# Three of four k-groups by seven products, two of the block sums added by accumulating loads

## The chip, the cores and the metric

The kernel runs on one core of one Trainium2 chip. The time is device microseconds (us) of one execution of the whole program; the median of three executions of the kernel before is 2425.75 us (2423.84 to 2429.18). The engines of the core are TensorE (PE, with its weight loads as PEld), VectorE (DVE), ScalarE (ACT), GpSimd (POOL) and SyncE (SP, which here only issues DMAs).

## The reference

Two transformer blocks follow each other on x of 256 tokens by 2048, all in float32. The two feed-forward networks (FFN) are what matters here; each has a hidden width of 5632 = 11 chunks of 512:

```python
def conv_ffn(x, w_gate, w_up, conv_w, conv_b, w_down):       # first block
    hg = x @ w_gate
    hg = causal_depthwise_conv(hg, conv_w, width=3) + conv_b
    return (jax.nn.gelu(hg, approximate=True) * (x @ w_up)) @ w_down

x = x + (jax.nn.silu(h @ w_gate[l]) * (h @ w_up[l])) @ w_down[l]   # second block
```

Before them stand the projections, the mixers and the output projections of each block, behind the first FFN a gated projection, and at the end a norm.

## The kernel before

**Precision.** A float32 product is made of three matmuls of a type with a shorter mantissa. Each 512 KB weight block (128 partitions by 1024) is loaded raw, ACT writes its rounded half `whi` (L133 or L603), and DVE the rest `wlo = raw - whi` (L134 or L604). PE then runs whi, wlo and whi again against the high and low halves of the activations. `whi` and `wlo` have five buffers each, so the split of a block waits until PE has used the block five before it. The raw blocks lie in three buffers `raw` and four buffers `t4k`; `load_weight` (L102) issues their loads on SP's queue in order.

**Tiling.** One block covers KG = 2 tiles of 128 of the contraction and 512 columns. The 256 tokens are two halves of 128. A plain product of a block is 2 (k tiles) x 2 (token halves) x 3 = 12 matmuls of 512 columns.

**Seven products for eight.** `pair_product` (L607) makes the gate and the up chunk `u` together. The 2048 of the contraction are 16 tiles, or four k-groups: group gp takes the blocks gp and gp + 4 of both weights, b11, b12 (gate and up of gp) and b21, b22 (gate and up of gp + 4). Eight block products of a half of the tokens (8 x 6 = 48 matmuls) can be made as seven (42 matmuls) out of sums of blocks, in the way of Strassen and Winograd: t1 = b11 + b12, t2 = t1 + b22, t3 = b12 + b22, t4 = t2 + b21. The products and their banks are p1 (b11), p2 (b21), q3 (b22), q5 (t1), q7 (t3), q6 (t2) and q4 (t4); the eight-bank PSUM is full while they run. DVE makes the four sums (L648, L652, L659, L662). The groups in MIXED = (0, 2) go this way, groups 1 and 3 plainly. The activations' own sums (`strassen_operands`, L570) are made once in each FFN. Chunks 0 and 1 are made plainly (`product`).

**Order of the work.** `ffn` (L731) goes over groups of chunks, (0, 1), (2, 3) ... (8, 9), (10): a chunk is made, and behind it stands half of the down products of the chunk group before (`drain`). The hidden activations of a chunk (16 transposes and the gating, `fill`) run as side work: each `pump()` in `product` emits a step of it. `pair_product` has no pump. A scheduler orders each engine's instructions; `tc.high_priority()` moves splits and sums ahead.

**After the groups** p1, q6, q5 and q7 are combined and p2, q3, q4 and x22 added (L672 to L679).

Of the kernel before, what the change touches and what calls it, by code (L numbers as in the profile page):

```python
# [14 lines left out]
ALU = mybir.AluOpType  # L15
# [8 lines left out]
KG = 2  # L24
# [29 lines left out]
def two_blocks_kernel(ctx: ExitStack, tc: tile.TileContext, A: dict, out: bass.AP):  # L54
# [12 lines left out]
    def t2k():  # L67
        return new([P, 512], "t2k", 8)
# [7 lines left out]
    def chunk_tile(dt=F32):  # L76
        return new([P, 2, 512], "pj", 8, dt)

    def psum(tag="tp"):
        return ps.tile([P, 512], F32, tag=tag, bufs=4, name=f"{tag}_{next(uid)}")  # L80
# [21 lines left out]
    def load_weight(w, c, g):  # L102
        deep = ahead[0] and next(loads) % 7 > 2
        raw = new([P, KG * 512], "t4k", 4) if deep else new([P, KG * 512], "raw", 3)
        nc.sync.dma_start(raw[:, : KG * w.widths[c]], w.block(c, g))
        return raw
# [35 lines left out]
    def add_side(gen, after=0):  # L142
        side.append([tick[0] + after, gen])
# [452 lines left out]
        add_side(make(), 1)  # L596
        return sx

    MIXED = (0, 2)

    def split_raw(raw):
        hi, lo = new([P, KG * 512], "whi", 5, F32R), new([P, KG * 512], "wlo", 5, F32R)
        act(hi, raw, AF.Copy)  # L603
        dve.tensor_tensor(lo, raw, hi.bitcast(F32), op=ALU.subtract)  # L604
        return hi, lo

    def pair_product(wa, wb, u, xs, sx):  # L607

        p1, q5, p2, q3 = (psum("acc") for _ in range(4))
        q6, q7, x22, q4 = (psum() for _ in range(4))
        ca, cb = chunk_tile(), chunk_tile()
        add, sub = ALU.add, ALU.subtract
        begun = set()

        def products(bank, st, wt, stop):
            (shi, slo), (hi, lo) = st, wt
            for j in range(KG):
                wh, wl = hi[:, j * 512 : (j + 1) * 512], lo[:, j * 512 : (j + 1) * 512]  # L620
                pe.matmul(bank, shi(j), wh, start=id(bank) not in begun, stop=False)  # L621
                begun.add(id(bank))
                pe.matmul(bank, shi(j), wl, start=False, stop=False)  # L623
                pe.matmul(bank, slo(j), wh, start=False, stop=stop and j == KG - 1)  # L624

        def plain(g, m):
            tok = slice(m * P, (m + 1) * P)
            return lambda j: xs[g * KG + j][0][:, tok], lambda j: xs[g * KG + j][1][:, tok]

        def mixed(gp, i):  # L630
            fs = slice(i * P, (i + 1) * P)
            return lambda j: sx[gp * KG + j][:, 0, fs], lambda j: sx[gp * KG + j][:, 1, fs]

        half = KT // KG // 2
        for gp in range(half):
            if gp not in MIXED:
                for w_, banks in ((wa, (p2, q4)), (wb, (q3, x22))):
                    for g in (gp, gp + half):
                        wt = split_weight(w_, u, g)
                        for m in range(2):  # L640
                            products(banks[m], plain(g, m), wt, g == KT // KG - 1)
                continue
            last = gp == MIXED[-1]
            b11, b12, b21, b22 = (load_weight(w_, u, g) for g in (gp, gp + half) for w_ in (wa, wb))
            with tc.high_priority():
                f11 = split_raw(b11)
                t1 = b11
                dve.tensor_tensor(t1, b11, b12, op=ALU.add)  # L648
                f21 = split_raw(b21)
                f22 = split_raw(b22)  # L650
                t3 = b12
                dve.tensor_tensor(t3, b12, b22, op=ALU.add)  # L652
            products(p1, plain(gp, 0), f11, last)
            products(p2, plain(gp + half, 0), f21, gp == half - 1)
            products(q3, mixed(gp, 3), f22, gp == half - 1)
            with tc.high_priority():
                ft1 = split_raw(t1)
                t2 = b22
                dve.tensor_tensor(t2, t1, b22, op=ALU.add)  # L659
                ft3 = split_raw(t3)  # L660
                t4 = b21
                dve.tensor_tensor(t4, t2, b21, op=ALU.add)  # L662
            products(q5, mixed(gp, 0), ft1, last)
            products(q7, mixed(gp, 2), ft3, last)
            with tc.high_priority():
                ft2 = split_raw(t2)
            products(q6, mixed(gp, 1), ft2, last)
            with tc.high_priority():
                ft4 = split_raw(t4)
            products(q4, plain(gp + half, 1), ft4, gp == half - 1)  # L670
            if last:
                act(ca[:, 0], p1, AF.Copy)  # L672
                dve.tensor_tensor(ca[:, 1], ca[:, 0], q6, op=add)
                dve.scalar_tensor_tensor(cb[:, 0], ca[:, 1], -1.0, q5, ALU.mult, add)
                dve.tensor_tensor(ca[:, 1], ca[:, 1], q7, op=add)
                dve.tensor_tensor(cb[:, 1], cb[:, 0], q7, op=sub)

        for t, bank in ((ca[:, 0], p2), (cb[:, 0], q3), (ca[:, 1], q4), (cb[:, 1], x22)):
            dve.tensor_tensor(t, t, bank, op=add)  # L679
        return ca, cb  # L680

    def conv_unit(u, xs, r, sx):
        if sx is None:
            gt = evacuate(product(W["gate"], u, xs), r)
            ut = evacuate(product(W["up"], u, xs), r)
        else:
            gt, ut = pair_product(W["gate"], W["up"], u, xs, sx)
            for t in (gt, ut):
                for m in range(2):
                    act(t[:, m], t[:, m], AF.Copy, scale=r[:, m : m + 1])  # L690

        def hidden(kk):
            i = u * 4 + kk
            t = psum()
            fs = slice(kk * P, (kk + 1) * P)
            tg = transpose_pair([gt[:, m, fs] for m in range(2)], t)
            tu = transpose_pair([ut[:, m, fs] for m in range(2)], t[:, T:])
            cv = t1k()
            act(cv, tg, AF.Identity, scale=CONV[2][:, i : i + 1], bias=CONVB[:, i : i + 1])
            dve.scalar_tensor_tensor(cv[:, 1:], tg[:, : T - 1], CONV[1][:, i : i + 1], cv[:, 1:], ALU.mult, ALU.add)  # L700
            dve.scalar_tensor_tensor(cv[:, 2:], tg[:, : T - 2], CONV[0][:, i : i + 1], cv[:, 2:], ALU.mult, ALU.add)
            act(cv, cv, AF.Gelu_apprx_tanh)
            dve.tensor_tensor(cv, cv, tu, op=ALU.mult)
            return stationary(cv, "hid")

        return hidden

    def swiglu_unit(u, xs, r, sx):
        if sx is None:
            sg = evacuate(product(W["gate2"], u, xs), r, func=AF.Silu)  # L710
            up = product(W["up2"], u, xs)
        else:
            sg, ut = pair_product(W["gate2"], W["up2"], u, xs, sx)
            for m in range(2):
                act(sg[:, m], sg[:, m], AF.Silu, scale=r[:, m : m + 1])
            up = [ut[:, m] for m in range(2)]
        for m in range(2):
            dve.scalar_tensor_tensor(sg[:, m], up[m], r[:, m : m + 1], sg[:, m], ALU.mult, ALU.mult)

        def hidden(kk):  # L720
            return stationary(transpose_pair([sg[:, m, kk * P : (kk + 1) * P] for m in range(2)]), "hid")

        return hidden

    def fill(hid, o, hidden):
        yield 1
        for kk in range(4):
            hid[o + kk] = hidden(kk)
            yield 1

    def ffn(unit, down, xs, r, g):  # L731

        groups = [(0, 1), (2, 3), (4, 5), (6, 7), (8, 9), (10,)]
        prev = None
        st = NormState() if g is not None else None
        sx = strassen_operands(xs)

        def drain(u0, hid, chunks, last=False):
            for c in chunks:
                add_to_h(c, product(down, c, hid, k0=u0 * 4))  # L740
                if last:
                    add_side(norm_chunk(c, g, st), 1)

        for us in groups:
            hid = [None] * (4 * len(us))
            for i, u in enumerate(us):
                add_side(fill(hid, 4 * i, unit(u, xs, r, sx if u > 1 else None)))
                if prev is not None:
                    step = NCH // len(us)
                    drain(*prev, range(i * step, (i + 1) * step))  # L750
            prev = (us[0], hid)
        if g is None:
            return final_rows(down, *prev)
        drain(*prev, range(NCH), True)
        return st.xs, st.r
# [440 lines left out]
```

## Time and profile before

| what | value |
|---|---|
| median of 3 executions | 2425.75 us |
| the profiled execution's own time | 2426.8 us |
| its span, first to last instruction | 2425.0 us |
| PE busy | 2392.8 us, 99% |
| DVE busy | 1804.9 us, 74% |
| ACT busy | 1352.7 us, 56% |
| POOL busy | 20.8 us, 1% |
| one chunk of the first FFN with its half drain | about 65 us |

The page gives busy shares of each engine, the chain of work that ended last, and groups of instructions. Matmuls overlap in the records, so their spacing, not their duration, is what one costs. A busy DVE block instruction is 1.22 us long in the records, but two back to back start 1.14 us apart.

### The profile page before, as it was taken

How to read it: one execution, taken by the hardware profiler on the slowest of the kernel's cores; microseconds unless marked ns; L12 is line 12 of the kernel's file. 1: busy time of each engine (PE TensorE's matmuls, PEld its weight loads, DVE VectorE, ACT ScalarE, POOL GpSimd, SP SyncE). 2: the span in 40 equal slices, each digit the busy share in tenths (PEclk: the TensorE clock that was granted, in tenths of full speed). 3: DMA queues.
4: the chain of work that ended last, by engine and by line, in shares of the span. 5: the costliest groups of instructions: out<-in, count | busy, mean ns of one | idle time of the engine just before them, and what ended most of it. 6: DMA issues, size and time to landing. Idle time of an engine off the chain costs nothing.

```text
span 2425.0 us, 30323 instructions
## 1 busy us (share of the span) xinstructions
PE 2392.8 (99%) x11208; PEld 1976.6 (82%) x11208; DVE 1804.9 (74%) x2223; ACT 1352.7 (56%) x1855; POOL 20.8 (1%) x26
## 2 busy tenths in 40 slices
PE   8999999999999999999999999999999999999998
PEld 7878888888788888888888888778888888888887
DVE  6786565668899888887656754655668888888885
ACT  6545455556566665565556554655545555555553
POOL 0000000000000000000000000000000000000000
PEclk9999999999999999999999999999999999999999
DMA  7544555556555555556545465545555555555553
GB/s 243 149 140 159 172 190 198 187 165 208 181 194 197 182 184 188 193 208 209 179 158 172 149 208 187 172 146 183 194 174 208 189 192 193 197 202 208 208 208 126
DMA packets 130659, 448.88 MB, mean 185 GB/s; under 512 B 14861, under 2 KB 19853, under 8 KB 130511
## 3 DMA queue, kind: packets, MB, share of 16 engines
q1 hardware_dynamic: 130510, 446.95, 54.9%
q8 instruction: 88, 1.44, 0.2%
q14 instruction: 61, 0.49, 0.1%
HBM read 444.76 MB, written 2.13 MB: 184 GB/s over the span
## 4 chain that ended last, share of the span: by engine, by line
PE 94%; DVE 3%; issue 1%; ACT 1%; DMA 1%; POOL 0%; SPq 0%; POOLq 0%; DVEq 0%; ACTq 0%
PE acc L156 19%; PE acc L158 19%; PE acc L157 19%; PE acc L621 5%; PE acc L623 5%; PE acc L624 5%; PE tp L623 5%; PE tp L621 5%; PE tp L624 5%; PE tp L195 2%; DVE wlo L134 1%; ACT whi L133 1%; DVE t2k L982 0%; DMA raw<-in_w_down 0%; PE tp L373 0%
## 5 line engine op out<-in xcount | busy, mean ns | idle before, releaser
L134 DVE TENSOR_TENSOR wlo<-raw,whi 128x1024 fp32r<-128x1024 f32 (+3 forms) x421 | 498.0, 1185 | 320.8 <-ACT whi L133 316.2
L133 ACT ACTIVATE whi<-raw 128x1024 fp32r<-128x1024 f32 (+3 forms) x421 | 433.0, 1029 | 417.3 <-PE acc L158 262.5
L156 PE MATMUL acc<-whi,xT 128*128 128x512 f32 (+3 forms) x1248 | 484.3, 388 | 0.0
L157 PE MATMUL acc<-wlo,xT 128*128 128x512 f32 (+3 forms) x1248 | 475.9, 381 | 0.0
L158 PE MATMUL acc<-whi,xT 128*128 128x512 f32 (+3 forms) x1248 | 475.9, 381 | 0.0
L134 DVE TENSOR_TENSOR wlo<-t4k,whi 128x1024 fp32r<-128x1024 f32 x271 | 330.6, 1224 | 175.1 <-ACT whi L133 170.1
L133 ACT ACTIVATE whi<-t4k 128x1024 fp32r<-128x1024 f32 x271 | 287.6, 1061 | 264.6 <-PE acc L158 147.0
L156 PE MATMUL acc<-whi,hid 128*128 128x512 f32 x944 | 377.8, 400 | 5.7 <-ACT hid L184 5.7
L157 PE MATMUL acc<-wlo,hid 128*128 128x512 f32 x952 | 371.8, 391 | 0.0
L158 PE MATMUL acc<-whi,hid 128*128 128x512 f32 x944 | 369.0, 392 | 0.0
L158 PEld LDWEIGHTS acc<-whi,xT 128*128 128x128 f32 x1248 | 235.4, 189 | 45.1 <-issue 0.9
L156 PEld LDWEIGHTS acc<-whi,xT 128*128 128x128 f32 x1248 | 235.6, 189 | 44.1 <-issue 3.2
L157 PEld LDWEIGHTS acc<-wlo,xT 128*128 128x128 f32 x1248 | 235.9, 189 | 42.5 <-DVE wlo L134 1.2
L603 ACT ACTIVATE whi<-t4k 128x1024 fp32r<-128x1024 f32 x143 | 151.8, 1061 | 139.0 <-PE acc L158 60.2
L156 PEld LDWEIGHTS acc<-whi,hid 128*128 128x128 f32 x944 | 177.6, 188 | 41.7 <-ACT hid L184 7.3
L158 PEld LDWEIGHTS acc<-whi,hid 128*128 128x128 f32 x944 | 177.5, 188 | 39.3 <-DVE hid L185 0.5
L157 PEld LDWEIGHTS acc<-wlo,hid 128*128 128x128 f32 x952 | 179.5, 189 | 34.7
L604 DVE TENSOR_TENSOR wlo<-t4k,whi 128x1024 fp32r<-128x1024 f32 x143 | 173.4, 1222 | 20.3 <-ACT whi L603 18.0
L603 ACT ACTIVATE whi<-raw 128x1024 fp32r<-128x1024 f32 x109 | 115.7, 1062 | 107.8 <-PE acc L158 46.9
L621 PE MATMUL acc<-whi,xT 128*128 128x512 f32 x432 | 168.1, 389 | 0.0
L623 PE MATMUL acc<-wlo,xT 128*128 128x512 f32 x432 | 168.1, 389 | 0.0
L624 PE MATMUL acc<-whi,xT 128*128 128x512 f32 x432 | 168.1, 389 | 0.0
(294 smaller groups left out, 3175.1 us busy)
## 6 DMA issues: line engine op xcount, KB each, us to landing
raw<-in_w_in SPq DMA_DIRECT2D x184, 512.0 KB, 3.6
t4k<-in_w_gate SPq DMA_DIRECT2D x100, 512.0 KB, 4.2
t4k<-in_w_up SPq DMA_DIRECT2D x100, 512.0 KB, 3.6
t4k<-in_w_down SPq DMA_DIRECT2D x96, 512.0 KB, 5.1
raw<-in_w_down SPq DMA_DIRECT2D x80, 512.0 KB, 5.1
raw<-in_w_gate SPq DMA_DIRECT2D x76, 512.0 KB, 3.9
raw<-in_w_up SPq DMA_DIRECT2D x76, 512.0 KB, 3.6
t4k<-in_w_out SPq DMA_DIRECT2D x37, 512.0 KB, 3.5
```

What stands on the lines that cost most here:

```text
L133: act(hi[:, :n], raw[:, :n], AF.Copy)
L134: dve.tensor_tensor(lo[:, :n], raw[:, :n], hi[:, :n].bitcast(F32), op=ALU.subtract)
L156: pe.matmul(o, xhi[:, tok], wh, start=first, stop=False)
L157: pe.matmul(o, xhi[:, tok], wl, start=False, stop=False)
L158: pe.matmul(o, xlo[:, tok], wh, start=False, stop=last)
L195: pe.transpose(t[:, m * P : (m + 1) * P], v, ident)
L603: act(hi, raw, AF.Copy)
L604: dve.tensor_tensor(lo, raw, hi.bitcast(F32), op=ALU.subtract)
L621: pe.matmul(bank, shi(j), wh, start=id(bank) not in begun, stop=False)
L623: pe.matmul(bank, shi(j), wl, start=False, stop=False)
L624: pe.matmul(bank, slo(j), wh, start=False, stop=stop and j == KG - 1)
```

## The change

MIXED becomes (0, 1, 2): three of four groups go by seven products. Chunk 1 is now made by `pair_product` too, and only chunk 0 plainly. Of the four sums DVE keeps t2 and t4. The sums t3 and t1 are made by DMAs on POOL's queue that load a block of the up weight from memory and add it to the block that lies in the buffer: t3 on top of b12, and t1 on top of b11 once f11, the split of b11, has read it. The products run in the order p1, p2, q3, q7, q5, q6, q4. The banks change places: p1, q6, q5 and q7 stand in the tag `tp`, which the side work uses too, and p2, q4, q3 and x22 in `acc`. In the last group `pump(1)` emits side work. The results lie in four tiles of `t2k` and not in `pj`.

```diff
-    MIXED = (0, 2)
+    MIXED = (0, 1, 2)
...
+        while any(k not in sx for gp in MIXED for k in range(gp * KG, gp * KG + KG)):
+            pump()
+
+        p1, q6, q5, q7 = (psum() for _ in range(4))
+        p2, q4, q3, x22 = (psum("acc") for _ in range(4))
...
+                        if gp > MIXED[-1]:
+                            pump(1)
...
+            t1, t2, t3, t4 = b11, b22, b12, b21
+
+            nc.gpsimd.dma_start(t3, wb.block(u, gp + half), accum_op=add)
             with tc.high_priority():
                 f11 = split_raw(b11)
-                t1 = b11
-                dve.tensor_tensor(t1, b11, b12, op=ALU.add)
+            nc.gpsimd.dma_start(t1, wb.block(u, gp), accum_op=add)
+            with tc.high_priority():
                 f21 = split_raw(b21)
                 f22 = split_raw(b22)
-                t3 = b12
-                dve.tensor_tensor(t3, b12, b22, op=ALU.add)
             products(p1, plain(gp, 0), f11, last)
             products(p2, plain(gp + half, 0), f21, gp == half - 1)
             products(q3, mixed(gp, 3), f22, gp == half - 1)
             with tc.high_priority():
+                ft3 = split_raw(t3)
                 ft1 = split_raw(t1)
-                t2 = b22
-                dve.tensor_tensor(t2, t1, b22, op=ALU.add)
-                ft3 = split_raw(t3)
-                t4 = b21
-                dve.tensor_tensor(t4, t2, b21, op=ALU.add)
+                dve.tensor_tensor(t2, t1, b22, op=add)
+            products(q7, mixed(gp, 2), ft3, last)
             products(q5, mixed(gp, 0), ft1, last)
-            products(q7, mixed(gp, 2), ft3, last)
             with tc.high_priority():
+                dve.tensor_tensor(t4, t2, b21, op=add)
                 ft2 = split_raw(t2)
...
-        groups = [(0, 1), (2, 3), (4, 5), (6, 7), (8, 9), (10,)]
+        groups = [(0,), (1, 2), (3, 4), (5, 6), (7, 8)] + ([(9, 10)] if g is not None else [(9,), (10,)])
...
-                add_side(fill(hid, 4 * i, unit(u, xs, r, sx if u > 1 else None)))
+                add_side(fill(hid, 4 * i, unit(u, xs, r, sx if u else None), u > 0))
```

In the new file t3's load stands on L651, t1's on L654, the sum t2 on L664 and t4 on L668. Before, DVE's queue in the second mixed group of chunk 4 of the first FFN (L604 is a split, the others are sums) reads:

```order
L604 TENSOR_TENSOR wlo_1429_6116<-raw_1424_6107,whi_1428_6115 128x1024
L648 TENSOR_TENSOR raw_1424_6107<-raw_1424_6107,raw_1425_6109 128x1024
L604 TENSOR_TENSOR wlo_1431_6121<-t4k_1426_6111,whi_1430_6120 128x1024
L604 TENSOR_TENSOR wlo_1433_6125<-t4k_1427_6113,whi_1432_6124 128x1024
L652 TENSOR_TENSOR raw_1425_6109<-raw_1425_6109,t4k_1427_6113 128x1024
L604 TENSOR_TENSOR wlo_1435_6148<-raw_1424_6107,whi_1434_6147 128x1024
L659 TENSOR_TENSOR t4k_1427_6113<-raw_1424_6107,t4k_1427_6113 128x1024
L662 TENSOR_TENSOR t4k_1426_6111<-t4k_1427_6113,t4k_1426_6111 128x1024
L604 TENSOR_TENSOR wlo_1437_6153<-raw_1425_6109,whi_1436_6152 128x1024
L604 TENSOR_TENSOR wlo_1439_6170<-t4k_1427_6113,whi_1438_6169 128x1024
L604 TENSOR_TENSOR wlo_1441_6180<-t4k_1426_6111,whi_1440_6179 128x1024
```

Seven splits and four sums stand between the products of one group. Now, DVE's queue in the second mixed group of the same chunk (L556 adds a down product to h):

```order
L604 TENSOR_TENSOR wlo_1467_6144<-t4k_1462_6134,whi_1466_6143 128x1024
L556 TENSOR_TENSOR h1_3_68<-h1_3_68,acc_1419_5954 128x512
L604 TENSOR_TENSOR wlo_1469_6149<-t4k_1464_6138,whi_1468_6148 128x1024
L604 TENSOR_TENSOR wlo_1471_6153<-raw_1465_6140,whi_1470_6152 128x1024
L604 TENSOR_TENSOR wlo_1473_6175<-t4k_1463_6136,whi_1472_6174 128x1024
L664 TENSOR_TENSOR raw_1465_6140<-t4k_1462_6134,raw_1465_6140 128x1024
L604 TENSOR_TENSOR wlo_1475_6179<-t4k_1462_6134,whi_1474_6178 128x1024
L668 TENSOR_TENSOR t4k_1464_6138<-raw_1465_6140,t4k_1464_6138 128x1024
L604 TENSOR_TENSOR wlo_1477_6197<-raw_1465_6140,whi_1476_6196 128x1024
L604 TENSOR_TENSOR wlo_1479_6207<-t4k_1464_6138,whi_1478_6206 128x1024
```

Two sums are gone. Between the split of b11 (the first row) and t2 (L664), the first instruction that reads t1, stand three splits and one L556. On POOL's queue nothing stood in the FFNs before but small norms; now it holds six DMAs for each chunk made by `pair_product`. These are the ones of chunk 4 (raw_1445 and raw_1444 belong to the first mixed group, t4k_1463 and t4k_1462 to the second, raw_1481 and raw_1480 to the third):

```order
L651 DMA raw_1445_6054<-in_w_up 128x1024
L651 DMA t4k_1463_6136<-in_w_up 128x1024
L654 DMA raw_1444_6052<-in_w_up 128x1024
L654 DMA t4k_1462_6134<-in_w_up 128x1024
L651 DMA raw_1481_6218<-in_w_up 128x1024
L654 DMA raw_1480_6216<-in_w_up 128x1024
```

The second group's t3 stands ahead of the first group's t1, so the latter waits behind it; in the second and third group t1 is at its turn when its own waits are over.

## Rows read from the trace of the kernel before

**Rows 1.** Page: span, then busy us, share and instructions by engine.
```profile
span 2425.0 us, 30323 instructions
PE 2392.8 (99%) x11208; PEld 1976.6 (82%) x11208; DVE 1804.9 (74%) x2223; ACT 1352.7 (56%) x1855; POOL 20.8 (1%) x26
```

**Rows 2.** Page: chain that ended last, by engine.
```profile
PE 94%; DVE 3%; issue 1%; ACT 1%; DMA 1%; POOL 0%; SPq 0%; POOLq 0%; DVEq 0%; ACTq 0%
```

**Rows 3.** Windows: us, busy by engine (instructions), PE clock, DMA share, GB/s.
```profile
689.00:754.00 65.00, 65.00 (x296) 53.52 (x294) 57.99 (x68) 39.34 (x49) 0.00 (x0) 1.00 0.57 196
...
947.00:1012.00 65.00, 65.00 (x295) 53.58 (x295) 57.99 (x67) 39.60 (x48) 0.00 (x0) 1.00 0.55 195
...
2200.00:2265.00 65.00, 65.00 (x292) 53.65 (x291) 56.75 (x58) 35.60 (x38) 0.00 (x0) 1.00 0.56 194
```

**Rows 4.** Timeline, PE: start, length; 20 matmuls from first row to last.
```profile
691.21 0.39 PE L621 MATMUL tp<-whi,xT 128*128 128x512 f32 x1
...
695.52 0.39 PE L623 MATMUL acc<-wlo,xT 128*128 128x512 f32 x1
```

**Rows 5.** Timeline, DVE: splits back to back.
```profile
946.58 2.35 DVE L604 TENSOR_TENSOR wlo<-raw,whi 128x1024 fp32r<-128x1024 f32 x2
948.85 1.22 DVE L134 TENSOR_TENSOR wlo<-raw,whi 128x1024 fp32r<-128x1024 f32 x1
```

**Rows 6.** Timeline, ACT: splits, [idle before <-releaser].
```profile
973.59 1.07 ACT L133 ACTIVATE whi<-raw 128x1024 fp32r<-128x1024 f32 x1 [0.30 <-PE tp L624]
976.31 1.06 ACT L133 ACTIVATE whi<-raw 128x1024 fp32r<-128x1024 f32 x1 [1.65 <-PE tp L624]
979.03 1.06 ACT L133 ACTIVATE whi<-raw 128x1024 fp32r<-128x1024 f32 x1 [1.66 <-PE tp L624]
```

**Rows 7.** Page: DMA issues, KB each, median us from issue to landing.
```profile
t4k<-in_w_gate SPq DMA_DIRECT2D x100, 512.0 KB, 4.2
t4k<-in_w_up SPq DMA_DIRECT2D x100, 512.0 KB, 3.6
```

**Rows 8.** All loads of in_w_gate.
```profile
DMA to landing us min/median/max: 3.3/4.1/6.3
```

**Rows 9.** Windows of 10 and 11 us inside one chunk, columns as in Rows 3.
```profile
956.00:967.00 11.00, 11.00 (x50) 9.13 (x49) 10.15 (x9) 6.53 (x8) 0.00 (x0) 1.00 0.33 119
967.00:977.00 10.00, 10.00 (x45) 8.27 (x45) 9.87 (x11) 6.99 (x8) 0.00 (x0) 1.00 0.88 302
```

**Rows 10.** Groups by line, POOL: busy us, mean ns of one.
```profile
L231 POOL TENSOR_TENSOR rs<-ms,mhalf 128x1 f32<-128x1 f32 x2 | 1.1, 550 | 700.9 <-DVE ms L230 700.9
```

**Rows 11.** Waits of PE, 545 to 1260 us: total us, times, longest.
```profile
PE acc L156 <- ACT hid L184: 5.7, 2, 3.9
```

**Rows 12.** Windows: the chunk-0-and-1 stage, and PE's clock after the waits.
```profile
552.00:592.00 40.00, 40.00 (x178) 33.14 (x177) 34.39 (x33) 23.80 (x25) 0.00 (x0) 1.00 0.70 245
...
615.00:620.00 5.00, 3.98 (x11) 3.09 (x12) 3.46 (x7) 2.32 (x5) 0.00 (x0) 0.69 0.00 0
```

More of the change, by code (lines that the diff above doesn't have):

```diff
@@ L607, in pair_product @@
     def pair_product(wa, wb, u, xs, sx):
-        p1, q5, p2, q3 = (psum("acc") for _ in range(4))
-        q6, q7, x22, q4 = (psum() for _ in range(4))
-        ca, cb = chunk_tile(), chunk_tile()
+        while any(k not in sx for gp in MIXED for k in range(gp * KG, gp * KG + KG)):
+            pump()
+        p1, q6, q5, q7 = (psum() for _ in range(4))
+        p2, q4, q3, x22 = (psum("acc") for _ in range(4))
         add, sub = ALU.add, ALU.subtract
@@ L671, in pair_product @@
             if last:
[L672 to L678, printed above, removed]
+                ca, cb = [t2k(), t2k()], [t2k(), t2k()]
+                act(ca[0], p1, AF.Copy)
+                dve.tensor_tensor(ca[1], ca[0], q6, op=add)
+                dve.scalar_tensor_tensor(cb[0], ca[1], -1.0, q5, ALU.mult, add)
+                dve.tensor_tensor(ca[1], ca[1], q7, op=add)
+                dve.tensor_tensor(cb[1], cb[0], q7, op=sub)
+        for t, bank in ((ca[0], p2), (ca[1], q4), (cb[0], q3), (cb[1], x22)):
             dve.tensor_tensor(t, t, bank, op=add)
@@ L683, in conv_unit @@
         if sx is None:
-            gt = evacuate(product(W["gate"], u, xs), r)
-            ut = evacuate(product(W["up"], u, xs), r)
+            gt, ut = (evacuate(product(W[n], u, xs), r) for n in ("gate", "up"))
+            gt, ut = ([t[:, m] for m in range(2)] for t in (gt, ut))
         else:
@@ L689, in conv_unit @@
                 for m in range(2):
-                    act(t[:, m], t[:, m], AF.Copy, scale=r[:, m : m + 1])
+                    act(t[m], t[m], AF.Copy, scale=r[:, m : m + 1])
         def hidden(kk):
@@ L695, in hidden @@
             fs = slice(kk * P, (kk + 1) * P)
-            tg = transpose_pair([gt[:, m, fs] for m in range(2)], t)
-            tu = transpose_pair([ut[:, m, fs] for m in range(2)], t[:, T:])
+            tg = transpose_pair([gt[m][:, fs] for m in range(2)], t)
+            tu = transpose_pair([ut[m][:, fs] for m in range(2)], t[:, T:])
             cv = t1k()
@@ L710, in swiglu_unit, with fill @@
             sg = evacuate(product(W["gate2"], u, xs), r, func=AF.Silu)
+            sg = [sg[:, m] for m in range(2)]
             up = product(W["up2"], u, xs)
         else:
-            sg, ut = pair_product(W["gate2"], W["up2"], u, xs, sx)
+            sg, up = pair_product(W["gate2"], W["up2"], u, xs, sx)
             for m in range(2):
-                act(sg[:, m], sg[:, m], AF.Silu, scale=r[:, m : m + 1])
-            up = [ut[:, m] for m in range(2)]
+                act(sg[m], sg[m], AF.Silu, scale=r[:, m : m + 1])
         for m in range(2):
-            dve.scalar_tensor_tensor(sg[:, m], up[m], r[:, m : m + 1], sg[:, m], ALU.mult, ALU.mult)
+            dve.scalar_tensor_tensor(sg[m], up[m], r[:, m : m + 1], sg[m], ALU.mult, ALU.mult)
         def hidden(kk):
-            return stationary(transpose_pair([sg[:, m, kk * P : (kk + 1) * P] for m in range(2)]), "hid")
+            return stationary(transpose_pair([sg[m][:, kk * P : (kk + 1) * P] for m in range(2)]), "hid")
         return hidden
-    def fill(hid, o, hidden):
-        yield 1
+    def fill(hid, o, hidden, wait):
+        if wait:
+            yield 1
         for kk in range(4):
```

## The prediction

> **What bounds the kernel now.** I read the page's busy shares first. PE is busy 99% of the span, DVE 74%, ACT 56% [rows 1], and the chain that ended last runs 94% on PE [rows 2]. A busy PE need not be PE at its peak, so the windows and the timeline come next. In a chunk of either FFN, PE has no idle time at full clock, while DVE is busy 58.0 us of 65 in the first FFN and 56.8 of 65 in the second [rows 3]. Twenty matmuls in a row start between 691.21 and 695.52: 4.31 / 19 = 0.227 us each [rows 4]. ACT's splits come every 2.72 us, each after a wait that PE ended [rows 6]: 12 matmuls x 0.227 = 2.72, so ACT waits for PE to free a `whi` buffer. Splitting runs as far ahead as five buffers allow, and PE is the bound. Only at the first chunk pair does PE wait for hidden activations, 5.7 us [rows 11], after which the granted clock falls to a mean of 0.69 for 5 us [rows 12].
>
> **The change part by part.**
>
> *Matmuls.* Each group that goes by seven products saves 6 matmuls. Before, 9 chunks had 2 such groups (18), now 10 chunks have 3 (30), in each FFN. (30 - 18) x 2 x 6 = 144 matmuls x 0.227 = 32.7 us. All stand on the path, since PE is it. The drains keep their matmuls, because the 44 hidden tiles are the same however the chunks are grouped.
>
> *DVE's work.* Before, a chunk needs 2 x (7 splits + 4 sums) + 8 plain splits = 30 block instructions; now 3 x (7 + 2) + 4 = 31. Back to back one costs (948.85 - 946.58) / 2 = 1.14 us [rows 5], so DVE does 58.0 + 1.1 = 59.1 us in a chunk that takes PE 65 - 6 x 0.227 = 63.6. There is room, on average. The chunk pair (1, 2) has half the drain behind it and is tighter, by at most 1 or 2 us a chunk; I leave that to the range. The second FFN's one added chunk group costs 8 adds to h on DVE, beside PE's drain. The activations' sums of two more k tiles fall into chunk 0, where DVE is idle 5.6 us in 40 [rows 12]. ACT gains 3 splits of 1.06 on 39.6 busy us of 65: nothing. These edits I cost at nothing; their cover is PE's matmuls, and where the cover goes, the next part says so.
>
> *The accumulating load of t1.* This is the new wait. t1 can be added only when f11 has been split, and DVE's queue then holds just three more splits before t2, which reads t1. Everything behind t2 on DVE (the splits ft1, ft2, ft4 and the next group's f11) waits with it, and PE's q5, q6, q4 wait for those. Call L the time from the end of f11's split to t1's landing. t3 does not matter: b12 is loaded long before it is wanted, and t3 is read first after three other splits. In the first group of a chunk, POOL holds t1 behind the second group's t3, but the blocks ahead are drain blocks of 2.72 us each, so f11 is split about 8 us before PE reaches the group; that covers it.
>
> Let PE start a chunk at 0. A group is 42 x 0.227 = 9.53 us, a product 1.36. In group 1, ft1's buffer comes free at 0 and its split starts 0.3 us later [rows 6]. After its ACT half (1.06), DVE does ft1, the sum t4, ft2, ft4 and the next f11: 0.3 + 1.06 + 5 x 1.14 = 7.1. So the second t1 lands at 7.1 + L. Then follow on DVE t2, ft1, t4, ft2, ft4 and the third f11, 6 x 1.14 = 6.8: 13.9 + L. The third t1 lands at 13.9 + 2L, and the third ft2 is split after t2, ft1, t4, ft2, at 18.5 + 2L. PE wants it for the second matmul of q6, at 2 x 9.53 + 5 x 1.36 + 0.23 = 26.1. PE therefore loses 2L - 7.6 = 2 x (L - 3.8) us in each chunk if L exceeds 3.8, and nothing below. In the plain group and the drain that follow, DVE catches up.
>
> What is L? The trace shows no accumulating load. The nearest rows are the plain loads of the same size in the same stage: medians 4.2 and 3.6 us from issue to landing [rows 7], least 3.3, most 6.3 [rows 8]. By 3.3 the loss is zero; by 6.3 it is 5.0 us a chunk, 100 us for 20 chunks. I take 4.2, the slower of the medians, since the load meets others of the next groups: 0.4 x 2 = 0.8 us a chunk, 16 us in all. POOL's issue could add to this; its smallest instruction takes 0.55 us [rows 10], which would bring L to 4.75 and the loss to 38 us.
>
> [...]
>
> *The other loads.* SP issues as many loads as before. The next group's b22 takes the buffer of t1, after ft1; DVE has t4, ft2, ft4, f11 and f21 to do (5.7 us, less 1.06 for the ACT half) before it wants it, against 4.2 for the load. SP's queue is in order, so loads behind it slip too if this one does. A group now moves 6 blocks of 0.524 MB in 9.53 us, 330 GB/s; the densest window moved 302 at a share of 0.88 [rows 9], 343 at full share. It fits, with 4% to spare, and seven buffers of lead.
>
> *The sum.* -32.7 + 16 = -16.7 us. From the profiled execution's own 2426.8 us (its span is 2425.0, the rest 1.8 lies around it) that gives **2410 us**. The median of the runs shown is 1.0 below the profiled execution, so the same sum on it is 2409.
>
> **The rivals.**
>
> *A: the accumulating load moves its bytes twice, and the change is slower.* It must read what lies in the buffer as well as the weight. Moving 0.524 MB at 343 GB/s takes 1.53 us [rows 9]; a second pass makes L 4.2 + 1.5 = 5.7, the loss 3.8 us a chunk or 76 us, and the time 2426.8 - 32.7 + 76 = 2470. The mechanism decides from L = 3.8 + 32.7 / 40 = 4.6 on. Counted so, a group moves 8 blocks, 12.2 us at 343 GB/s against PE's 9.53, which speaks for late loads as well. For it: nothing in the trace shows an add on the way to be free. Against it: the engines' DMA share is 0.55 on the mean of a chunk [rows 3], so one block more may find idle engines.
>
> [...]
>
> *B: L stays under 3.8.* The load of t1 then lands like the quickest plain ones (3.3), nothing is lost, and 2426.8 - 32.7 = 2394. Against it: medians of 3.6 to 4.2 belong to loads that start beside fewer others.
>
> *C: no change.* L between 4.5 and 4.75 eats what the matmuls save: 2422 to 2432.
>
> *D: DVE takes over as the bound.* At 59.1 of 63.6 us it would need bubbles of 4.5 us a chunk. Chunk by chunk that is the same event as L, so I give it no chance of its own. The wait at the first chunk pair (5.7 us and the lower clock after it) may go or come back elsewhere, since the hidden tiles of chunk 0 are now emitted in its last group: some 7 us either way, inside the range.
>
> **How the numbers follow.** Forecast (L from 3.9 to 4.5, 2398 to 2422): 0.40. Rival A: 0.36. B: 0.14. C: 0.10. The cases of both signs hold much of the chance, so the forecast's own range of 2398 to 2422 stands beside the whole one, 2394 to 2470, which reaches from B to A and leaves out L over 5.7 and a lost wait at the first pair on top of B. Faster by over 0.2% (about what a measurement of this kernel can tell from no change, 5 us): 0.40 + 0.14 = 0.54; within it 0.10; slower 0.36.
>
> **What would show it.** The matmul step: PE's instructions fall by 144, and their spacing stays 0.227. The load: DMA issues of POOL with 120 rows, and a median to landing near 4 us; at 5.5 or more, rival A. The wait: t2 (L664) waits on a DMA, about 1 us in the second and third group of a chunk and hardly in the first; PE then waits for splits in the third group. If t2 never waits, B; if PE waits 4 us and more in each chunk, A. DVE should be busy about 59 us in a chunk. The forecast is wrong if the loads of gate and up come later than 6 us or if PE waits at another place, as at a bank that side work holds.

## The result, and the profile after

The changed kernel takes 2592.22 us (median of 4 runs, 2585.93 to 2604.62) against 2425.64 of the kernel before: a ratio of 1.0691, 95% interval 1.0674 to 1.0707. It is 167 us slower, where 16 us faster was forecast, and beyond the upper end of the range, 2470.

The profiled execution took 2604.62 us, its span is 2602.8. The page of the changed kernel, busy us by engine, then the chain that ended last [rows 1, 2]:

```profile
PE 2450.7 (94%) x11064; PEld 1985.4 (76%) x11064; DVE 1865.0 (72%) x2323; ACT 1417.8 (54%) x1933; POOL 126.5 (5%) x146
...
PE 56%; DMA 19%; DVE 14%; issue 8%; ACT 3%; POOL 0%; POOLq 0%; DVEq 0%; SPq 0%; ACTq 0%
```

The 144 matmuls are gone (11208 to 11064). Yet PE, idle for 32 us before, is idle for 152, and 19% of the chain is DMA, which was 1%. The waits of PE and of DVE in the changed kernel say whose (us in total, times, longest); the second fence is DVE's:

```profile
PE tp L623 <- ACT whi L603: 71.5, 36, 3.7
PE tp L625 <- DVE wlo L604: 42.5, 55, 4.6
```
```profile
DVE t4k L664 <- DMA raw<-in_w_up: 87.2, 25, 8.7
DVE raw L664 <- DMA t4k<-in_w_up: 83.1, 24, 5.5
DVE t4k L664 <- DMA t4k<-in_w_up: 25.7, 8, 4.6
```

L664 is t2, the sum that reads t1. It waited 57 times of 60 for t1's load, 196.0 us in all, 3.4 each. That DVE waits here is what the prediction named. PE waits for splits of `tp` products; counted in PE's timeline by their place in the group, 98 us of these waits stand at the first two matmuls of q5, which reads t1, and 7 us at the second of q6, where the prediction had the wait. The size of t2's wait is in the loads' own rows. First the page's queues (packets, MB, share of 16 engines' span) and the two kinds of POOL's loads (count, KB, median us to landing), then t1's line L654:

```profile
q1 hardware_dynamic: 130510, 446.95, 51.3%
q0 software_dynamic: 17280, 62.92, 13.9%
...
t4k<-in_w_up POOLq DMA_DIRECT2D x69, 512.0 KB, 7.4
raw<-in_w_up POOLq DMA_DIRECT2D x51, 512.0 KB, 7.2
```
```profile
DMA to landing us min/median/max: 5.5/7.2/9.5
```

The plain loads land in 3.6 and 4.2 us [rows 7]; t1's take 7.2, and the least of them (5.5) lies well above the plain median of 4.1 [rows 8]. One megabyte on POOL's queue q0 takes 13.9 / 62.92 = 0.22% of the engines, on SP's q1 51.3 / 446.95 = 0.115%: per megabyte an accumulating load occupies them 1.9 times as long.

One second group, in DVE's and POOL's timelines (start, length, [idle before <- releaser]):

```profile
926.32 2.48 DVE L604 TENSOR_TENSOR wlo<-t4k,whi 128x1024 fp32r<-128x1024 f32 x2
928.72 0.68 DVE L556 TENSOR_TENSOR h<-h,acc 128x512 f32<-128x512 f32 x1
929.32 3.51 DVE L604 TENSOR_TENSOR wlo<-raw,whi 128x1024 fp32r<-128x1024 f32 x3
936.91 1.23 DVE L664 TENSOR_TENSOR raw<-t4k,raw 128x1024 f32<-128x1024 f32 x1 [4.08 <-DMA t4k<-in_w_up]
938.05 1.22 DVE L604 TENSOR_TENSOR wlo<-t4k,whi 128x1024 fp32r<-128x1024 f32 x1
```
```profile
929.21 0.87 POOL L654 DMA_DIRECT2D t4k<-in_w_up  x1 [15.11 <-DVE wlo L604]
```

The first row ends with the split of f11, at 926.32 + 2.48 = 928.80. POOL issues t1's load 0.4 us later, DVE makes the three splits f21, f22, ft3 that its queue still holds, and then stands for 4.08 us, until t1 has landed: L = 936.91 - 928.80 = 8.1 here, and 0.4 + 7.2 = 7.6 by the median landing. The prediction took 4.2.

What PE does then, in windows of 5 us (PE, PEld, DVE, ACT, POOL busy, PE clock, DMA share, GB/s) [rows 12]:

```profile
935.00:940.00 5.00, 3.44 (x15) 2.31 (x14) 3.09 (x3) 2.11 (x2) 0.00 (x0) 1.00 0.65 181
940.00:945.00 5.00, 4.61 (x15) 3.20 (x14) 4.93 (x5) 4.48 (x5) 0.62 (x1) 0.66 0.71 227
...
950.00:955.00 5.00, 2.45 (x9) 1.44 (x8) 3.41 (x3) 2.11 (x2) 0.00 (x0) 0.92 0.30 104
955.00:960.00 5.00, 5.00 (x18) 3.97 (x17) 4.93 (x6) 4.80 (x6) 0.00 (x0) 0.73 0.75 238
```

PE is idle 1.56 + 0.39 us in the second group and 2.55 in the third, and behind these waits the granted clock falls to a lower level for a while: 0.66 and 0.73 on the mean of 5 us, 0.50 in windows of 1 us (941 to 944 and 955 to 957). The wait of the third group in PE's timeline, at the first two matmuls of q5:

```profile
952.69 0.50 PE L623 MATMUL tp<-whi,pj 128*128 128x512 f32 x1 [1.73 <-ACT whi L603]
954.01 0.62 PE L625 MATMUL tp<-wlo,pj 128*128 128x512 f32 x1 [0.82 <-DVE wlo L604]
```

Over the span the mean clock is 0.971, against 0.997 before. With 0.50 as the lower level that is, as an estimate, 2602.8 x 0.029 x 2 = 151 us there instead of 15. The part on why the prediction was wrong prices it.

### The profile page after: what moved, and what is told of

It reads as the page before. It is cut to its first block, busy times and chain, and to the rows that moved or that the text cites. A ratio compares the mean times of both kernels' runs of the same rounds, so it can differ in the third digit from the quotient of the medians.

```text
span 2602.8 us, 30730 instructions
## 1 busy us (share of the span) xinstructions
PE 2450.7 (94%) x11064; PEld 1985.4 (76%) x11064; DVE 1865.0 (72%) x2323; ACT 1417.8 (54%) x1933; POOL 126.5 (5%) x146
## 3 DMA queue, kind: packets, MB, share of 16 engines
q1 hardware_dynamic: 130510, 446.95, 51.3%
q0 software_dynamic: 17280, 62.92, 13.9%
## 4 chain that ended last, share of the span: by engine, by line
PE 56%; DMA 19%; DVE 14%; issue 8%; ACT 3%; POOL 0%; POOLq 0%; DVEq 0%; SPq 0%; ACTq 0%
PE acc L156 13%; PE acc L158 13%; PE acc L157 13%; DMA t4k<-in_w_up 11%; DMA raw<-in_w_up 7%; DVE wlo L604 6%; PE acc L623 3%; PE acc L625 3%; PE acc L626 3%; DVE wlo L134 2%; PE tp L195 2%; PE tp L625 1%; ACT whi L603 1%; ACT whi L133 1%; PE tp L626 1%
## 5 line engine op out<-in xcount | busy, mean ns | idle before, releaser
L134 DVE TENSOR_TENSOR wlo<-raw,whi 128x1024 fp32r<-128x1024 f32 (+3 forms) x380 | 446.4, 1180 | 282.6 <-ACT whi L133 281.2
L156 PE MATMUL acc<-whi,xT 128*128 128x512 f32 (+3 forms) x1120 | 433.5, 387 | 0.0
L158 PE MATMUL acc<-whi,xT 128*128 128x512 f32 (+3 forms) x1120 | 425.7, 380 | 0.0
L157 PE MATMUL acc<-wlo,xT 128*128 128x512 f32 (+3 forms) x1120 | 425.6, 380 | 0.0
L604 DVE TENSOR_TENSOR wlo<-t4k,whi 128x1024 fp32r<-128x1024 f32 x239 | 287.0, 1220 | 25.7 <-ACT whi L603 23.8
L603 ACT ACTIVATE whi<-raw 128x1024 fp32r<-128x1024 f32 x181 | 190.0, 1058 | 195.0 <-DMA raw<-in_w_up 103.7
L156 PEld LDWEIGHTS acc<-whi,xT 128*128 128x128 f32 x1120 | 211.5, 189 | 39.5 <-issue 3.2
L158 PEld LDWEIGHTS acc<-whi,xT 128*128 128x128 f32 x1120 | 211.2, 189 | 40.0 <-issue 0.9
L623 PE MATMUL tp<-whi,pj 128*128 128x512 f32 x360 | 164.3, 456 | 74.4 <-ACT whi L603 69.9
L604 DVE TENSOR_TENSOR wlo<-raw,whi 128x1024 fp32r<-128x1024 f32 x181 | 218.4, 1220 | 19.8 <-ACT whi L603 18.5
L623 PE MATMUL acc<-whi,xT 128*128 128x512 f32 x560 | 222.0, 397 | 2.9 <-ACT whi L603 2.9
L625 PE MATMUL acc<-wlo,xT 128*128 128x512 f32 x560 | 220.4, 394 | 1.9 <-DVE wlo L604 1.8
L626 PE MATMUL acc<-whi,xT 128*128 128x512 f32 x560 | 219.2, 391 | 0.0
L625 PE MATMUL tp<-wlo,pj 128*128 128x512 f32 x360 | 171.5, 476 | 42.2 <-DVE wlo L604 41.7
```

Of the source, the lines that this page charges most:

```text
L134: dve.tensor_tensor(lo[:, :n], raw[:, :n], hi[:, :n].bitcast(F32), op=ALU.subtract)
L156: pe.matmul(o, xhi[:, tok], wh, start=first, stop=False)
L157: pe.matmul(o, xhi[:, tok], wl, start=False, stop=False)
L158: pe.matmul(o, xlo[:, tok], wh, start=False, stop=last)
```

## The experiments

Each kernel is the changed one with an edit, unless it says otherwise; times are medians, ratios are to the kernel before. Theory 1: the time from f11's split to t1's landing costs what the prediction's formula says, only longer. Theory 2: DVE is the bound inside the groups. The rival of both: the accumulating loads burden the DMA engines, which makes all loads late. Six kernels leave out one or both of the additions of t1 and t3, so that they do not compute the reference and only show what a part costs: no_add, free_sums, t3_load_alone, t1_load_alone, ten_on_dve and spread_no_load.

**t3_only**

```diff
-            nc.gpsimd.dma_start(t1, wb.block(u, gp), accum_op=add)
-                dve.tensor_tensor(t2, t1, b22, op=add)
+                dve.tensor_tensor(t2, b11, t3, op=add)
+                dve.tensor_tensor(t1, t2, b22, op=sub)   # ahead of ft1
```

> Three groups and both orders of work as in the changed kernel, but only t3 by an accumulating load; t2 = b11 + t3 and t1 = t2 - b22 on DVE, so no sum waits for a load that could start only after a split. DVE does 34 block instructions a chunk (58.0 + 4 x 1.14 = 62.6 us against PE's 63.6). Theory 1 (the latency of t1's load, behind DVE's queue, costs PE all of it): the waits go, 2394 to 2430, likeliest 2405. Rival (accumulating loads weigh on the DMA engines, which makes all loads late): half of them stay, so half of the loss stays, about 2490. Second rival (DVE is the bound at 34): PE waits for DVE without any DMA behind it, 2430 or more.

2497.86, 1.0303 (1.0288 to 1.0318). The waits for DMA are nearly gone (DVE waits 9.3 us for t3, in 4 waits), yet some 100 us of the 2394 are lost. Theory 1 alone fails: PE now waits 57 times for ACT's halves of splits. Of the expectations the second rival held, DVE as the bound.

**t3_on_dve**

```diff
-            nc.gpsimd.dma_start(t3, wb.block(u, gp + half), accum_op=add)
                 f22 = split_raw(b22)
+                dve.tensor_tensor(t3, b12, b22, op=add)
```

> The mirror: t3 on DVE, only t1 by an accumulating load. Theory 1: the wait of t2 on t1 stays in every group, so the time stays: 2570 to 2630, rather above the changed kernel's 2592 than below, since DVE has three instructions more a chunk, but these also fill part of its wait. Rival (load of the DMA engines): half the loss goes, about 2490.

2599.02, 1.0718 (1.0693 to 1.0744): t1's load alone, with one more DVE instruction a group, is as slow as the whole change, as theory 1 has it. But ten_on_dve below prices the one instruction at 71 us, so this run does not show it by itself; t1_load_alone does.

**both_on_dve**

```diff
-            nc.gpsimd.dma_start(t3, ...); nc.gpsimd.dma_start(t1, ...)
+                dve.tensor_tensor(t1, b11, b12, op=add)   # behind f11
+                dve.tensor_tensor(t3, b12, b22, op=add)   # behind f22
```

> No accumulating load at all; three groups, chunk 1 by seven products, grouping and banks as in the changed kernel. DVE does 37 block instructions a chunk: 58.0 + 8.0 = 66.0 us in the first FFN and 56.8 + 8.0 = 64.7 in the second, above PE's 63.6. Both theories on the loads: 2394 + 10 x 2.4 + 10 x 1.1 = about 2430 (2400 to 2460). If it comes out near 2590 the loads were not the cause, and the new order or the banks were.

2532.09, 1.0438 (1.0422 to 1.0453): 100 us more than I expected of a kernel without any such load. What I had summed over a chunk happens in a group: 11 DVE instructions x 1.14 = 12.5 us against PE's 9.53, three times in a row. That is argued here; ten_on_dve tests it. Of PE's waits 23.9 us are for banks of the drain, which DVE's adds free late.

**no_add**

```diff
-            nc.gpsimd.dma_start(t1, wb.block(u, gp), accum_op=add)
+            nc.gpsimd.dma_start(t1, wb.block(u, gp))          # t3 likewise
```

> The 120 loads of GpSimd's queue stay where they are but do not add (t1 and t3 are then plain copies of the up weight's blocks, so the sums are not computed). Prices the add against the queue. If the add costs the second pass over 0.524 MB (packets of 328 ns instead of 159), landing falls from 7.2 us to about 5, L to about 6, and with 2 x (L - 3.8) and half as much again for the clock the time is 2500 to 2540. If the queue of GpSimd is all of it: landing stays near 7, 2580 to 2600. If the add is all of it: landing near 4.4, 2410 to 2440.

2460.34, 1.0141 (1.0124 to 1.0158). POOL's queue, a plain load of SP's and POOL's loads of this kernel:

```profile
q0 software_dynamic: 17280, 62.92, 7.5%
...
t4k<-in_w_gate SPq DMA_DIRECT2D x100, 512.0 KB, 4.3
...
t4k<-in_w_up POOLq DMA_DIRECT2D x69, 512.0 KB, 4.9
raw<-in_w_up POOLq DMA_DIRECT2D x51, 512.0 KB, 4.8
```

The same packets and bytes take 7.5% of the engines instead of 13.9%, and land in 4.8 to 4.9 us instead of 7.2 to 7.4: the add costs 2.4 us. GpSimd's queue without the add costs 0.5 to 0.7 over SP's loads (4.3 in this kernel, 4.1 before [rows 8]). In engine time the add costs as much as the second pass of rival A would: 13.9% of the changed kernel's span of 2602.8 us against 7.5% of 2459.8 here is 1.96 times. What the engines do in that time no run shows. Less was lost than expected since L is 5.2, not 6, and the granted clock stayed at 0.998.

**free_sums**

```diff
-            nc.gpsimd.dma_start(t3, ...)
-            nc.gpsimd.dma_start(t1, ...)
```

> The changed kernel without its 120 accumulating loads: t1 and t3 are then b11 and b12 alone (the up weight is not added to them). The matmuls, splits, t2, t4, banks and order stay. It is the case L = 0 and shows what the rest of the change costs. Theory 1 (only the wait on t1 costs): 2394, at most 2400. Theory 2 (DVE's density: inside a seven-product group DVE has 9 block instructions, 9 x 1.14 = 10.3 us, against 9.53 us of PE, with 10 in t3_only and 11 in both_on_dve; three groups in a row use up the lead of five buffers): 3 x 0.7 = 2.2 us a chunk, nearly all inside the lead, 2394 to 2415. Rival (banks and order of the change cost by themselves): 2430 or more.

2396.52, 0.9877 (0.9862 to 0.9892): with L = 0 the change saves 30 us. That is the matmuls' 32.7 less 3, so order, banks, grouping and DVE's 9 instructions a group cost next to nothing together, and PE is busy 99% again:

```profile
PE 2361.0 (99%) x11064; PEld 1947.5 (81%) x11064; DVE 1864.5 (78%) x2323; ACT 1422.9 (59%) x1933; POOL 20.8 (1%) x26
```

**interleaved**

```diff
+            if not last:
+                plain_block(gp)      # one of the four plain blocks behind groups 0 and 1
```

> The changed kernel with the four plain blocks of group 3 put elsewhere: one behind the first seven-product group, one behind the second, two behind the third. Both accumulating loads stay. Theory 1 and 2 together: a plain block gives DVE 2.72 - 1.14 = 1.6 us of lead back twice a chunk, so the loss of 2 x (8.1 - 3.8) = 8.6 us a chunk falls to about 5.4, with the half clock 2500 to 2560. If the place of the groups does not matter: 2592.

2571.31, 1.0615 (1.0589 to 1.0640): 21 us better, not 30 to 90. PE now also waits for banks of the drain (16.3 us), so part of the lead that the plain blocks give may have been spent there; no run shows it.

**t3_interleaved**: the edits of t3_only and interleaved together.

> The same places of the plain blocks with only t3 accumulated (t2 = b11 + t3, t1 = t2 - b22 on DVE). Theory 2 (density): 10 block instructions are 11.4 us against 9.53, 1.9 short in each group, of which 1.6 comes back in the plain block: the loss of t3_only (2498) goes almost wholly, 2394 to 2430, likeliest 2410. If DVE's sum over the whole chunk is what binds (34 instructions, 62.6 us of 63.6): little gained, 2460 to 2500. If the accumulating loads weigh by their traffic: 2490.

2607.32, 1.0740 (1.0723 to 1.0758), a miss: slower than t3_only. PE's first wait shows why; L690 adds the last products to the result and so frees the banks that the drain wants:

```profile
PE acc L156 <- DVE t2k L690: 111.3, 19, 12.2
```

With two plain blocks instead of four behind the last group, DVE's adds, in line behind the splits, come too late; t3_interleaved_b below tests this reading.

**late_t1**

```diff
+                dve.tensor_tensor(t2, b11, t3, op=add)    # behind ft3
+            nc.gpsimd.dma_start(t1, wb.block(u, gp), accum_op=add)
...
+            plain_block(gp)
+                ft1 = split_raw(t1)
+            products(q5, mixed(gp, 0), ft1, last)
```

> Both sums by accumulating loads, DVE at 31 block instructions a chunk, but t2 = b11 + t3 (so no sum waits for t1), t1's load issued behind t2, and q5, the one product of t1, made last, behind the plain block that follows its group. From t2's end to ft1's place in DVE's queue stand t4, the splits ft2, ft4, f22 and a plain block, 5 x 1.14 = 5.7 us, and DVE's lead of five blocks on top. Theory 1: the 7.2 us to landing are hidden, 2394 to 2415. Rival (the traffic of loads that weigh double makes gate's and up's loads late): 2450 or more, with SP and DVE waiting for plain loads.

2506.75, 1.0329 (1.0314 to 1.0345). No sum on DVE waits for a DMA any more (ACT now does for the split of t1, 110 us, not all of it on the path), and 85 of 196 us come back. 55 us of PE's waits are for banks, as in t3_interleaved.

**late_t1b**

```diff
+        p1, q5, p2, q3 = (psum("acc") for _ in range(4))
+            products(q7, mixed(gp, 2), ft3, last)
+            if gp:
+                product_t1(gp - 1)                        # ft1 and q5 of the group before
```

> late_t1 (2507) with its two waits taken away. First, t1's split and product q5 go further back, behind f11, f21, ft3 and t2 of the next group (in late_t1 ACT stood 5 us at ft1 behind a plain block). Second, the banks lie as in the kernel before (p1 and q5 are the first that the drain takes) and the combining adds go ahead of the drain's splits (PE waited 55 us there). Theory 1: 2507 - 55 of bank waits - some 17 of PE's waits for splits - up to 20 of half clock = 2415; if the place of the groups and the cover fit everywhere, down to 2397. Faster than the kernel before: better than even. Rival (traffic of double-weight loads): no lower than 2450.

2524.22, 1.0400 (1.0384 to 1.0415), a miss. The plain loads land late, as they already did in late_t1 (gate's t4k in 5.2, up's in 5.4; in free_sums in 4.0 to 4.2). New is that ACT waits for gate's, 64.5 us against 2.7 in late_t1 (second fence, one of ACT's waits):

```profile
t4k<-in_w_gate SPq DMA_DIRECT2D x102, 512.0 KB, 5.4
t4k<-in_w_up SPq DMA_DIRECT2D x98, 512.0 KB, 5.4
```
```profile
ACT whi L603 <- DMA raw<-in_w_gate: 37.2, 16, 5.5
```

So the late plain loads that the rival expects are there in both kernels. Whether the traffic makes them late, or t1 by holding its buffer longer, so that SP fills the next one later, no run took apart.

**t3_interleaved_b**: t3_interleaved with the banks and the earlier adds of late_t1b.

> t3_interleaved (2607) with banks and combining adds as in late_t1b. If its 111 us of PE waiting for the drain's banks were the whole reason why it got slower than t3_only, it falls to about 2607 - 111 - 8 - half of 150 us of half clock = 2410 to 2440. If DVE's 34 instructions a chunk are the bound, 2450 to 2500.

2508.65, 1.0328 (1.0311 to 1.0345): 99 us come back, so the bank waits were most of what t3_interleaved lost against t3_only, but it is no better than t3_only (2498). Why the plain blocks between groups did not pay stays open.

**pool_sums**

```diff
-            nc.gpsimd.dma_start(t1, wb.block(u, gp), accum_op=add)
+                pool.tensor_tensor(t1, b11, b12, op=add)
+                pool.tensor_tensor(t3, b12, b22, op=add)   # behind f22; t3's load goes
```

> No accumulating load: GpSimd's own ALU adds t1 and t3 in SBUF (products q5 and q7 in the order of the kernel before). DVE stays at 9 block instructions a group, as in free_sums (2396.5). Theory 1 (only the length of the step from f11's split to t1, against 3.8 us, and DVE's 9 instructions): if GpSimd's add of 128x1024 takes 3.5 us or less, 2396 to 2415, faster than the kernel before. No row so far shows such an add. [...] Rival: GpSimd's reads and DVE's two-input instructions hold each other up, DVE loses as much as GpSimd adds, and the time is that of both_on_dve (2532) or more; DVE's instructions would then be seen longer than 1.22 us.

2595.93, 1.0700 (1.0682 to 1.0718). Two of POOL's groups, then DVE's splits (busy us, mean ns of one):

```profile
L654 POOL TENSOR_TENSOR t4k<-t4k,t4k 128x1024 f32<-128x1024 f32 x25 | 82.0, 3281 | 432.6 <-DVE wlo L604 432.6
...
L658 POOL TENSOR_TENSOR t4k<-t4k,t4k 128x1024 f32<-128x1024 f32 x18 | 50.8, 2822 | 1.4
```
```profile
L604 DVE TENSOR_TENSOR wlo<-t4k,whi 128x1024 fp32r<-128x1024 f32 x239 | 352.6, 1494 | 35.1 <-ACT whi L603 33.2
L604 DVE TENSOR_TENSOR wlo<-raw,whi 128x1024 fp32r<-128x1024 f32 x181 | 271.5, 1517 | 34.6 <-ACT whi L603 33.2
```

t1's add takes 3.3 us here, within the 3.5 that the expectation set, but the two adds stand in line on POOL, and DVE's splits are 1.49 and 1.52 us long instead of 1.22: 239 x 0.27 + 181 x 0.30 = 119 us more on the engine with no room. The two causes were not taken apart. The splits are 22 to 24% longer than the 1.22 us of free_sums, where GpSimd makes no sum; so much of the rival the rows show, but not what makes them longer.

**t3_acc_pool_t1**

```diff
+                dve.tensor_tensor(t2, b11, t3, op=add)
+                pool.tensor_tensor(t1, t2, b22, op=sub)
+            products(q5, mixed(gp, 0), ft1, last)          # behind q4
```

> t3 by the accumulating load (early, nobody waits), t2 = b11 + t3 on DVE, t1 = t2 - b22 on GpSimd's ALU, and q5 made last in its group. One GpSimd add a group instead of two, DVE at 9. Theory 1: 2396 to 2420 if t3 lands before its split; against t3_only (2498) the only thing taken away is one DVE instruction a group. Rival (DVE and GpSimd hold each other up): between 2450 and 2500. Rival (t3's 7 us to landing are exposed when the buffers turn over): DVE's sum t2 is seen to wait for a DMA, 2430 or more.

2528.05, 1.0424 (1.0408 to 1.0439): the rival of longer DVE instructions again; the splits of L604 are 1.37 us long on the mean, and GpSimd's subtraction takes 3.4 to 4.1.

**t3_load_alone**: only t1's load is left out. **t1_load_alone**: only t3's.

> The changed kernel without t1's load (t1 is then b11 alone); t3 by its accumulating load, which may start long before it is wanted. Theory 1 (latency of t1's load alone): as free_sums, 2396 to 2405. Rival (traffic of the double-weight loads): about half the loss, 2490.

> The changed kernel without t3's load (t3 is then b12 alone); t1 by its accumulating load. Theory 1: nearly the whole loss stays; without t3's load behind it on the same queue t1 lands in some 5.8 us, as in t3_on_dve, instead of 7.2, so L falls by 1.4 and the loss by 2 x 1.4 x 20 = 56 us and some clock: 2500 to 2550. If the two loads only add up by traffic: 2490. If t3's load costs nothing at all, not even the queue: 2592.

2402.15, 0.9900 (0.9885 to 0.9915), and 2553.69, 1.0522 (1.0507 to 1.0536). Against free_sums t3's load costs some 6 us, t1's 157, both together 196. The two kernels load and add the same bytes, by POOL's queue of t3_load_alone, then of t1_load_alone, with t1's line there:

```profile
q0 software_dynamic: 8640, 31.46, 7.9%
```
```profile
q0 software_dynamic: 8640, 31.46, 7.5%
...
DMA to landing us min/median/max: 5.4/6.4/7.8
```

So in this order of work the traffic of an accumulating load, which is what the rival goes by, costs some 6 us; the 151 more come from what waits for t1's load. The 33 over the sum fit t1 landing later beside t3's loads, 7.2 us instead of 6.4: 40 x 0.8 = 32. Whether POOL's queue or the DMA engines hold it up, no run took apart.

**ten_on_dve**

```diff
-            nc.gpsimd.dma_start(t3, ...); nc.gpsimd.dma_start(t1, ...)
+                dve.tensor_tensor(t1, b11, b12, op=add)   # behind f11; t3 stays b12
```

> No load; t1 by DVE, t3 left as b12 alone: 10 DVE block instructions a group. Theory 2 (density against 9.53 us of PE, with a lead of five buffers): between free_sums with 9 (2397) and both_on_dve with 11 (2532), nearer the former because the lead covers the first part: 2420 to 2465. If the loss is in proportion: 2464. If the order of DVE's work (not its amount) made both_on_dve slow: 2397 to 2405.

2467.45, 1.0165 (1.0151 to 1.0179): one more DVE instruction a group costs 71 us, two cost 136 (both_on_dve). Three groups of n instructions give 3 x (n x 1.14 - 9.53) = 2.2, 5.6, 9.0 us a chunk for n = 9, 10, 11; less 2.1 for the lead that the buffers give, a figure chosen so that n = 9 costs nothing, this is 0.1, 3.5 and 6.9, or 2, 70 and 138 us for 20 chunks, against 0, 71 and 136 measured. What is tested are the two steps, 68 us each by the rule, 71 and 65 measured; 7 and 10 of these are matmuls at the lower clock, which the rule leaves out. The count is not all: t3_only, also with ten, lost 101.

**two_groups_on_dve**: both_on_dve with `MIXED = (0, 2)`.

> The part of the change that adds no density: MIXED (0, 2) with plain groups between, all four sums on DVE, no load, but chunk 1 by seven products, the new grouping, product order and banks. 2 chunks x 2 groups x 6 = 24 matmuls fewer than before, 24 x 0.227 = 5.4 us: 2420, a ratio of 0.998 to the kernel before. If the new order or banks cost when all sums are on DVE: 2430 or more.

2423.56, 0.9992 (0.9984 to 1.0001): 5.4 us were expected and at most 4 are there; no difference that could be told.

**spread** and **spread_no_load** (without t3's load). Here too t2 = b11 + t3 and t1 = t2 - b22 stand on DVE.

```diff
+            if not last:
+                plain_block(2 * gp)           # two plain blocks behind groups 0 and 1, none behind 2
+                plain_block(2 * gp + 1)
```

> Three groups with two plain blocks behind the first and two behind the second, so each group stands alone; t3 accumulated, t2 = b11 + t3 and t1 = t2 - b22 on DVE (10 instructions a group); banks as in the kernel before, combining adds ahead of the last product q4. By the rule with k = 1: 11.4 - 9.53 - 2.1 is below zero, no loss: 2396 + 6 for t3's load (t3_load_alone) = 2402, and up to 15 for bank waits at the chunk's end: 2402 to 2420, faster than the kernel before. If bank waits at the drain, now without plain blocks as cover, cost 2 us a chunk or more: 2440 or more.

> The same without t3's load (t3 is then b12 alone). If the load costs as little as in t3_load_alone, 6 us below spread. If spread is slow because t3 lands late in this layout, 2396 to 2410; if it is slow because of banks or DVE, as slow as spread.

2644.25, 1.0912 (1.0885 to 1.0939), and 2470.18, 1.0182 (1.0168 to 1.0196): both miss. In spread POOL's loads land in 8.3 to 8.6 us and t2, which here reads t3, waits for them, as in the first of four such rows of DVE's waits:

```profile
DVE t4k L668 <- DMA t4k<-in_w_up: 77.9, 20, 5.8
```

The load of t3, nearly free in t3_load_alone, costs 174 us here. My reading: t2 reads t3 and stands right behind f11 in DVE's queue, where in the changed kernel ft3, three splits later, is the first to read it; no run moved t2 alone. And spread_no_load loses 74 us against free_sums where the lead should have covered all: 27 us of PE's waits there are for sums on DVE at the end of a chunk, which the expectation of spread named as a risk, and the rest is not taken apart. So the rule of ten_on_dve holds for three groups in a row and was not shown for groups apart. No version that computes the reference beat the kernel before by more than can be told.

## Why the prediction was wrong, step by step

**The matmuls** were right: 144 fewer, 0.227 us apart still, and 30 us in free_sums against 32.7.

**DVE's work** at nothing was right for the 9 instructions a group that the change leaves (free_sums), but partly by luck. I compared 59.1 with 63.6 us over a chunk; what counts by ten_on_dve is 10.3 against 9.53 in a group, three times, less the lead. With one instruction more, 71 us were lost while the chunk's sum, 62.6 us, still fitted.

**t3 does not matter**: right, within some 6 us, in t3_load_alone; beside t1's load it added 39 (196 less 157), and t1 landed 0.8 us later.

**The formula** 2 x (L - 3.8) us a chunk was right, for the waits. L below is the 0.4 us before the issue, as read in the one group above, and the median landing of t1's line (4.8, 6.4, 7.2). The last three columns are counted over free_sums. "Waits" and "slow matmuls" are read from the starts of PE's matmuls in the profiled executions: where the granted clock is at its lower level, starts that follow each other without a wait lie 0.427 us apart instead of 0.227, and what that adds is "slow matmuls"; every other gap that grew is "waits".

| kernel | L, us | 40 x (L - 3.8) | mean clock | measured | waits | slow matmuls |
|---|---|---|---|---|---|---|
| free_sums | 0 | 0 | 0.998 | 0 | 0 | 0 |
| no_add | 5.2 | 56 | 0.998 | 64 | 62 | 2 |
| t1_load_alone | 6.8 | 120 | 0.979 | 157 | 116 | 40 |
| changed kernel | 7.6 | 152 | 0.971 | 196 | 149 | 59 |

The formula meets the waits within 6 us in all three. What comes on top are the matmuls at the lower clock. (The changed kernel's profiled execution is 12 us longer than the median, so its two parts add up to 208.) The prediction had no term for them.

The place was named wrong. The formula has PE wait for ft2, at the second matmul of q6; the waits stand at q5, for ft1, which ACT and DVE split as soon as t1 has landed and t2 is done. By the prediction's own times q5's second matmul wants ft1 at 24.7 and ft1 is split at 13.9 + 2L + 2.3, so 6.7 of the 7.6 us are already due there with L = 7.6. The sum does not change by it.

**L is the step that failed.** "I take 4.2, the slower of the medians" put an accumulating load of GpSimd's queue at the time of a plain load of SP's. It is 7.6: over the 4.1 of a plain load 0.4 us to the issue, 0.7 for the queue and 2.4 for the add. Rival A had twice the engine time (1.96 times, against no_add), but priced its second pass as bytes at 343 GB/s, worked from [rows 9] (1.5 us), and kept the 4.2 under it. With 7.6 the prediction's own sum is 2426.8 - 32.7 + 152 = 2546; the 44 left of the measured 196, which the slow matmuls cover, make it 2590.

**The range** failed with it. The end of 6.3 us came from plain loads, and even that end gave 100 us, 2494; I stopped at 2470. The slowest row of another kind of transfer bounds nothing.

**The first chunk pair**'s wait of 5.7 us [rows 11] went down to 0.9, as allowed for. Two waits of 4.2 us in all came for it, at a `tp` bank that side work holds (PE L623 behind DVE's L707), a place that the prediction had listed as a sign of being wrong; they are too small to matter.

## What to carry to other kernels

A transfer that the trace does not show should get a run that measures its parts (here 0.4 us to the issue, 4.8 to landing on its queue without the add, 2.4 for the add), not the median of its plain relatives; and where one formula turns a microsecond of latency into 40 of time, that number is the whole prediction. Ask of each new dependent load how many instructions the waiting queue still holds: here three splits, 3.4 us, against a step of 7.6. Compare an engine's work with the bound over the stretch that its buffers can bridge, not over the whole period.

## What the runs showed of the hardware

- In the changed kernel an accumulating load of 512 KB on GpSimd's queue landed in 7.2 us (median of t1's) and took 1.96 times the engine time of the same load without the add (no_add), which landed in 4.8; its packets took 328 ns, those of SP's plain loads 159 (medians); POOL was busy 0.87 us issuing it. The median differs from kernel to kernel: 5.6 to 5.7 us in t3_load_alone, 6.4 for t1's in t1_load_alone, 8.3 to 8.6 in spread.
- GpSimd's add of 128x1024 float32 took 2.8 to 3.4 us in pool_sums (by groups), and DVE's splits of L604 took 1.49 and 1.52 us on the mean there, against 1.22 in free_sums.
- Waits of PE of up to 4.6 us, a few in each chunk, went with a fall of the mean granted clock from 0.997 to 0.971, with 0.50 in windows of 1 us behind them; matmuls there started 0.427 us apart instead of 0.227, which took 59 us more than in free_sums, beside 149 us of waits.
